# Projections multiplied by parts, score matmuls in pairs, and a reordered forget mixer with its convolution rows ranked behind the weight rests

## The chip, the cores and the metric

The kernel runs on one core of one Trainium2 chip. The metric is the device time of one execution in microseconds (us). TensorE does the matmuls, VectorE, ScalarE and GpSimd the elementwise work, and SyncE issues most transfers.

## The reference

The reference takes 256 tokens of width 1024 through three mixers and four feed-forward blocks, all in float32. The parts that matter here are these:

```python
# first mixer: differential attention (4 heads, two maps each) beside a pooling mixer
proj = rms_norm(x, norm_g) @ w_in                 # 1024 x 2048: q, k, v, u
s = einsum('bqhmd,bkhmd->bhmqk', q, k) * scale + bias      # head width 64
p = softmax(s); attn = p[:, :, 0] - lam * p[:, :, 1]
# second mixer: sliding window attention, 16 q heads, 2 kv heads, width 64, with sinks
proj = rms_norm(x, norm_g) @ w_in                 # 1024 x 1280
# third mixer ("forget mixer"), after the third feed-forward block
a, g, q, k, v, fl = split(rms_norm_2(x, mix_norm) @ w_in)  # 1024 x 2568
u = a * sigmoid(g)
y_conv = silu(layer_norm(conv31(u) + conv_b))     # 31 taps per channel, 512 channels
cum = cumsum(log_sigmoid(fl + forget_b))
s = q @ k.T * scale + cum[query] - cum[key]       # 8 heads of width 64, causal
y_attn = softmax(s) @ v
x = x + concat(rms_norm_2(y_conv), rms_norm_2(y_attn)) @ w_out
# feed-forward blocks: up to 2 x 2816, (convolution of 3 taps in the first two,) silu(gate) * up, down
```

## The kernel before

Tokens lie in two blocks of 128 (tb 0 and 1). Weights stream from memory in tiles of 1 MB (128 x 2048) in the order in which they are used (class Stream). Two staging buffers (NSTAGE) take the transfers; ScalarE rounds a staged tile into "whi" (L218) and VectorE subtracts that from the staged tile, four chunks of 512 columns, into the rest "wlo" (L222). Five buffers (NBUF) hold split tiles; one comes free when its last matmul has been done. Every float32 product is made of three matmuls of rounded numbers: activation part times weight part as hi·hi, hi·rest and rest·hi (mm3). A projection (class Proj) multiplies one token block with 512 columns of the weights in two halves of four k-blocks each; a half's weights are one tile, one chunk to a k-block.

The code states an order of work, and a planner makes each engine's order out of it at compile time: an instruction's rank is its place in the program, and on each engine the ready instruction of the best rank goes first. `tc.high_priority(offset=-n)` ranks a block as if it stood n instructions later. The split of weights stands at LATER = 400, the convolution's row steps (conv_rows) at LATERC.

Scores: a matmul of 64 rows gives one head's scores for a token block in full float32; the profile shows it as two entries. Heads (or maps) 2b and 2b+1 lie in partitions 0 to 63 and 64 to 127 of the same block. softmax_rows collects several scores of one such half in one of four PSUM buffers (pps) and lets VectorE add the bias and take the row minimum (L635) into one of six buffers "t512" (TB). In the forget mixer the function `gate` adds the cumulated gates to the scores by one matmul (L1158) and one or two more (L1160), all of 128 rows, ahead of that.

Forget mixer: conv_in(j) makes the convolution's two inputs for 128 channels, Conv.gate their product. The 31 taps are row steps on VectorE (L1088 the first, L1090 the others; 113 in all) but for 11 taps of cv[1], which TensorE does as matmuls with a diagonal (L1105) and which L1108 joins. proj_qk(s, b) makes one block of 128 rows of q (s = 0) or k (s = 1): 24 matmuls (L521 to L523) and a copy (L1148); with b = 3 it frees two weight tiles. Then come scores, transposes (values_T), products with v (values), the norms, and the out-projection in parts op.part(tb, kk): kk 2 and 3 need the attention, 0 and 1 the convolution (conv_norm, L1196 to L1204, and mix_T, whose rest part is L290).

Of the kernel before, what the change touches and what calls it, by code (L numbers as in the profile page):

```python
# [14 lines left out]
ALU = mybir.AluOpType  # L15
# [4 lines left out]
S = 256  # L20
# [17 lines left out]
NPE = (0, 11, 0, 0)  # L38
LATERC = 300
VCOPY = {((1, 0), 4), ((0, 0), 4), ((0, 1), 2), ((1, 1), 0), ((1, 1), 6)}  # L40
# [69 lines left out]
def block_kernel(ctx: ExitStack, tc: tile.TileContext, a: dict, out: bass.AP):  # L110
# [158 lines left out]
    def mm3(o, l, r, first, last):  # L269

        T.matmul(o, l[0], r[0], start=first, stop=False)  # L271
        T.matmul(o, l[0], r[1], start=False, stop=False)  # L272
        T.matmul(o, l[1], r[0], start=False, stop=last)  # L273

    def cut(pair, *idx):
# [309 lines left out]
    class Proj:  # L585
# [5 lines left out]
        def half(self, h):  # L591
            if self.o is None:
                self.o = acc_t("proj")
            w = v3(W.get(self.wname, self.first + h), 4)
            rows_mm(self.o, xT, self.tb, w, range(4 * h, 4 * h + 4), h == 0, h == 1)
            W.used(self.wname, self.first + h)
# [25 lines left out]

    def softmax_rows(qT, kT, heads, tb, rel, nm, den, SP, extra=None):

        L = P * (tb + 1)
        per = 512 // L
        for i in range(0, len(heads), per):
            pst = ps_t("sc")
            Sx = t512("S")
            for n, (r0, qb, kb, slope, idx) in enumerate(heads[i:i + per]):  # L630
                o = pst[:, n * L:(n + 1) * L]
                T.matmul(o, qT[r0:r0 + 64, qb, :], kT[r0:r0 + 64, kb, 0:L], start=True, stop=extra is None)  # L632
                if extra is not None:
                    extra(o, idx, L)
                V.tensor_tensor_reduce(Sx[:, n * L:(n + 1) * L], o, rel[:, S - L:S], slope, 3e38,  # L635
                                       ALU.add, ALU.min, nm[:, idx:idx + 1])
                SP[idx] = Sx[:, n * L:(n + 1) * L]

# [5 lines left out]
    class AttendA:  # L644
# [5 lines left out]
        def scores(self, *hs):  # L650
            tb, SP, rd, den = self.tb, self.SP, self.rd, self.den
            for m in range(2):
                softmax_rows(qTA[:, :, tok(tb)], kTA, [(64 * m, h, h, SLOPES_A[h], 2 * h + m) for h in hs],
                             tb, C("rel"), self.nm, den, SP)
            exps([2 * h + m for m in range(2) for h in hs], SP, self.nm, den)
# [259 lines left out]
    class AttendC(Values):  # L915
# [4 lines left out]
        def scores(self, *blks):  # L920
            c, tb, SP, nm, den, sk = self.c, self.tb, self.SP, self.nm, self.den, self.sk
            kT1 = kTC[c].rearrange("p (o t) -> p o t", o=1)
            for e in range(2):
                softmax_rows(qTC[c][:, :, tok(tb)], kT1,
                             [(64 * e, b, 0, SLOPES_C[8 * c + 2 * b + e], 2 * b + e) for b in blks],
                             tb, C("relw"), nm, den, SP)
            i = slice(2 * blks[0], 2 * blks[-1] + 2)
# [224 lines left out]
    class AttendF(Values):  # L1152
# [10 lines left out]
        def scores(self, *blks):  # L1163
            for e in range(2):
                softmax_rows(q2[:, :, tok(self.tb)], k2, [(64 * e, b, b, 1.0, 2 * b + e) for b in blks],
                             self.tb, C("mask"), self.nm, self.den, self.SP, self.gate)
            exps([2 * b + e for e in range(2) for b in blks], self.SP, self.nm, self.den)
            i = slice(2 * blks[0], 2 * blks[-1] + 2)
            V.reciprocal(self.rd[:, i], self.den[:, i])
# [56 lines left out]
    conv_in(3)  # L1226
    conv_rows(cv[2])
    proj_qk(1, 2)
    proj_qk(1, 1)
    proj_qk(0, 2)  # L1230
    proj_qk(1, 0)
    proj_qk(0, 3)
    cv[3].gate()
    f1.scores(0, 1)
    conv_rows(cv[3])
    f0.scores(0, 1)
    proj_qk(1, 3)
# [135 lines left out]
```

## Time and profile before

| | us |
|---|---|
| runs | 1060.22, 1063.0, 4472.5 |
| median of these | 1063.0 |
| profiled execution | 1060.59 |
| its span, first to last instruction | 1058.7 |

The profile belongs to one execution. A line of it names the engine, the line of the kernel and the tiles written and read (out<-in). PE is TensorE, PEld its weight loads, DVE VectorE, ACT ScalarE, POOL GpSimd. L12 is line 12 of the kernel. The time of a matmul in these lines is its latency; matmuls overlap, so the distance between the starts of neighbours tells what one costs in a row. Idle time before an instruction stands in brackets with what ended it.

### The profile page before, as it was taken

The numbers are of one execution on the slowest core, as the hardware profiler recorded it, in microseconds if no ns is written. First come the engines' busy times: TensorE is split into PE (matmuls) and PEld (weight loads), VectorE is DVE, ScalarE is ACT, GpSimd is POOL, SyncE is SP. The second block draws the span as 40 slices with busy tenths as digits, with TensorE's granted clock in tenths as the row PEclk, the third lists the DMA queues.
The fourth block names the chain that finished last, engine by engine and source line by source line (L and its number), as shares of the span: only waits on it lengthen the run. The fifth ranks groups of instructions, "written<-read, shape, count | busy, mean of one in ns | idle before, by whom it ended". The sixth has DMA issues, their size and how long they took to land.

```text
span 1058.7 us, 15504 instructions
## 1 busy us (share of the span) xinstructions
PE 1040.9 (98%) x5873; PEld 892.1 (84%) x5873; DVE 779.4 (74%) x1694; ACT 622.2 (59%) x1119; POOL 32.1 (3%) x40
## 2 busy tenths in 40 slices
PE   8999999999999999999999999999999999999997
PEld 5778988888877798888889888888898888888885
DVE  6686788878867578888787666656799896656662
ACT  6485666666657456666665555554644566554552
POOL 1100000000011000000000000000000010000000
PEclk9999999999999999999999999999999999999999
DMA  7635566655453074665545655554613156655531
GB/s 268 235 139 199 179 202 206 229 176 182 159 179 115 5 243 144 223 209 197 199 159 182 226 181 188 199 190 169 224 54 120 46 214 223 215 176 189 192 119 40
DMA packets 28746, 185.17 MB, mean 175 GB/s; under 512 B 3320, under 2 KB 4224, under 8 KB 7552
## 3 DMA queue, kind: packets, MB, share of 16 engines
q1 hardware_dynamic: 28672, 184.19, 50.0%
q8 instruction: 46, 0.75, 0.3%
q14 instruction: 28, 0.23, 0.1%
HBM read 183.13 MB, written 1.05 MB: 174 GB/s over the span
## 4 chain that ended last, share of the span: by engine, by line
PE 86%; DVE 6%; DMA 3%; ACT 2%; POOL 1%; issue 1%; SPq 0%; POOLq 0%; ACTq 0%; DVEq 0%
PE up L529 26%; PE up L531 14%; PE dn L271 7%; PE dn L272 7%; PE dn L273 7%; DVE wlo L222 2%; PE sc L632 2%; DMA st<-in_w 2%; PE proj L273 2%; PE o L896 2%; PE proj L272 1%; PE op L271 1%; PE op L273 1%; PE op L272 1%; PE lead L273 1%; PE lead L271 1%
## 5 line engine op out<-in xcount | busy, mean ns | idle before, releaser
L222 DVE TENSOR_TENSOR wlo<-st,whi 128x512 fp32r<-128x512 f32 x668 | 433.1, 686 | 158.2 <-ACT whi L218 158.1
L218 ACT CAST whi<-st 128x1024 fp32r<-128x1024 f32 (+1 forms) x336 | 339.1, 1042 | 131.1 <-PE dn L273 29.7
L529 PE MATMUL up<-xT,whi 128*128 128x512 f32 x1216 | 303.9, 392 | 0.8 <-DVE c L461 0.7
L529 PEld LDWEIGHTS up<-xT,whi 128*128 128x128 f32 x1216 | 220.7, 189 | 42.0 <-PE up L431 1.2
L531 PEld LDWEIGHTS up<-xT,wlo 128*128 128x128 f32 x1216 | 165.9, 190 | 11.9
L531 PE MATMUL up<-xT,wlo 128*128 128x256 f32 x1216 | 169.5, 282 | 0.0
L271 PE MATMUL dn<-whi,g 128*128 128x512 f32 x352 | 137.5, 391 | 0.0
L272 PE MATMUL dn<-wlo,g 128*128 128x512 f32 x352 | 137.1, 390 | 0.0
L273 PE MATMUL dn<-whi,g 128*128 128x512 f32 x352 | 136.7, 389 | 0.0
L536 ACT COPY h<-up 128x256 f32<-128x256 f32 x152 | 55.6, 366 | 69.3 <-PE up L531 69.0
L273 PEld LDWEIGHTS dn<-whi,g 128*128 128x128 f32 x352 | 66.1, 188 | 14.2 <-DVE g L473 0.3
L271 PEld LDWEIGHTS dn<-whi,g 128*128 128x128 f32 x352 | 66.2, 188 | 13.0 <-ACT g L472 0.4
L272 PEld LDWEIGHTS dn<-wlo,g 128*128 128x128 f32 x352 | 66.3, 188 | 12.2
L472 ACT CAST g<-m 128x256 fp32r<-128x256 f32 x88 | 35.6, 406 | 64.4 <-DVE m L468 64.4
L537 DVE TENSOR_TENSOR h<-up,h 128x256 f32<-128x256 f32 x152 | 63.6, 418 | 11.5 <-ACT h L536 11.4
L271 PE MATMUL lead<-whi,xT 128*128 128x256 f32 x192 | 55.6, 289 | 0.0
L273 PE MATMUL lead<-whi,xT 128*128 128x256 f32 x192 | 54.3, 283 | 0.0
L272 PE MATMUL lead<-wlo,xT 128*128 128x256 f32 x192 | 54.3, 283 | 0.0
L456 ACT ACTIVATE c<-h,pv 128x256 f32<-128x256 f32 x76 | 45.6, 602 | 6.1 <-DVE h L537 6.1
L473 DVE TENSOR_TENSOR g<-m,g 128x256 fp32r<-128x256 f32 x88 | 36.9, 422 | 16.5 <-ACT g L472 13.7
L272 PE MATMUL proj<-wlo,xT 128*128 128x512 f32 x112 | 44.9, 403 | 2.4 <-DVE wlo L222 2.3
L271 PE MATMUL proj<-whi,xT 128*128 128x512 f32 x112 | 44.6, 403 | 2.0 <-ACT whi L218 1.8
(227 smaller groups left out, 1366.4 us busy)
## 6 DMA issues: line engine op xcount, KB each, us to landing
st<-in_up SPq DMA_DIRECT2D x88, 1024.0 KB, 4.8
st<-in_dn SPq DMA_DIRECT2D x44, 1024.0 KB, 4.8
st<-in_w SPq DMA_DIRECT2D x21, 1024.0 KB, 4.8
gb<-in_rows SPq DMA_DIRECT2D x9, 512.0 KB, 4.2
st<-in_w0o SPq DMA_DIRECT2D x4, 1024.0 KB, 4.8
st<-in_w1o SPq DMA_DIRECT2D x4, 1024.0 KB, 4.7
st<-in_w2o SPq DMA_DIRECT2D x4, 1024.0 KB, 4.8
st<-in_w SPq DMA_DIRECT2D x4, 256.0 KB, 5.6
```

Of the source, the lines that this page charges most:

```text
L218: A.copy(hi[:, c], st[:, c])
L222: V.tensor_sub(lo[:, c], st[:, c], hi[:, c].bitcast(F32))
L271: T.matmul(o, l[0], r[0], start=first, stop=False)
L272: T.matmul(o, l[0], r[1], start=False, stop=False)
L273: T.matmul(o, l[1], r[0], start=False, stop=last)
L456: A.activation(cs[s], hs[s], AF.Identity, bias=PVs(cb, blk), scale=PVs(cw, 3 * blk + 2))
L472: A.copy(hi, m)
L473: V.tensor_sub(lo, m, hi.bitcast(F32))
L529: T.matmul(o, w[0], xT.both(ko), start=ko == 0, stop=False, skip_group_check=True)
L531: T.matmul(o[:, :S], w[1], xT[0][:, ko, :], start=False, stop=ko == KD - 1, skip_group_check=True)
L536: A.copy(h, o[:, S:])
L537: V.tensor_tensor(h, o[:, :S], h, ALU.add)
```

## The change

Proj.half no longer goes through its k-blocks with three matmuls each; mm3s makes all hi·hi products of the half, then all with the rest of the activations, then all with the rest of the weights. softmax_rows takes pairs of heads that lie in different halves of the partitions, opens two PSUM buffers at once and issues the two score matmuls of a pair one behind the other, ahead of the gates and of VectorE's reduce steps; all three mixers use it. The rank offset of the convolution's rows grows from 300 to 700. In the forget mixer the scores of the first heads move between the products of q and k, f1.scores(0, 1) is split in two, and the rows of the last convolution block come behind f1.scores(1).

```diff
--- before.py
+++ after.py
@@ -36,7 +36,7 @@
 FIRST = {("w0", 0): 4, ("w0", 1): 2}
 TB, UB = 6, 5
 NPE = (0, 11, 0, 0)
-LATERC = 300
+LATERC = 700
 VCOPY = {((1, 0), 4), ((0, 0), 4), ((0, 1), 2), ((1, 1), 0), ((1, 1), 6)}
 O_PS = {(1, 0), (1, 1)}
 DENG = "AAAA"
@@ -271,6 +271,12 @@
         T.matmul(o, l[0], r[0], start=first, stop=False)
         T.matmul(o, l[0], r[1], start=False, stop=False)
         T.matmul(o, l[1], r[0], start=False, stop=last)
+
+    def mm3s(o, terms, first, last):
+
+        order = [(l[i], r[j]) for i, j in ((0, 0), (1, 0), (0, 1)) for l, r in terms]
+        for n, (l, r) in enumerate(order):
+            T.matmul(o, l, r, start=first and n == 0, stop=last and n == len(order) - 1)
 
     def cut(pair, *idx):
         return tuple(t[idx] for t in pair)
@@ -592,7 +598,8 @@
             if self.o is None:
                 self.o = acc_t("proj")
             w = v3(W.get(self.wname, self.first + h), 4)
-            rows_mm(self.o, xT, self.tb, w, range(4 * h, 4 * h + 4), h == 0, h == 1)
+            mm3s(self.o, [(cut(xT, slice(None), 4 * h + i, tok(self.tb)), cut(w, slice(None), i)) for i in range(4)],
+                 h == 0, h == 1)
             W.used(self.wname, self.first + h)
 
         def all(self):
@@ -620,21 +627,26 @@
         A.activation((qTA, kTA)[s][:, :, tok(tb)], transposes(hn.pop((s, tb)), 4).rearrange("p (b t) -> p b t", b=4),
                      AF.Copy, scale=(nqg, PVs("kg"))[s])
 
-    def softmax_rows(qT, kT, heads, tb, rel, nm, den, SP, extra=None):
+    def softmax_rows(qT, kT, pairs, tb, rel, nm, SP, extra=None):
+
 
         L = P * (tb + 1)
         per = 512 // L
-        for i in range(0, len(heads), per):
-            pst = ps_t("sc")
-            Sx = t512("S")
-            for n, (r0, qb, kb, slope, idx) in enumerate(heads[i:i + per]):
-                o = pst[:, n * L:(n + 1) * L]
-                T.matmul(o, qT[r0:r0 + 64, qb, :], kT[r0:r0 + 64, kb, 0:L], start=True, stop=extra is None)
-                if extra is not None:
-                    extra(o, idx, L)
-                V.tensor_tensor_reduce(Sx[:, n * L:(n + 1) * L], o, rel[:, S - L:S], slope, 3e38,
-                                       ALU.add, ALU.min, nm[:, idx:idx + 1])
-                SP[idx] = Sx[:, n * L:(n + 1) * L]
+        for i in range(0, len(pairs), per):
+            pst = [ps_t("sc") for _ in range(2)]
+            Sx = [t512("S") for _ in range(2)]
+            for n, pair in enumerate(pairs[i:i + per]):
+                at = slice(n * L, (n + 1) * L)
+                for e, (r0, qb, kb, slope, idx) in enumerate(pair):
+                    T.matmul(pst[e][:, at], qT[r0:r0 + 64, qb, :], kT[r0:r0 + 64, kb, 0:L], start=True,
+                             stop=extra is None)
+                for e, (r0, qb, kb, slope, idx) in enumerate(pair):
+                    o = pst[e][:, at]
+                    if extra is not None:
+                        extra(o, idx, L)
+                    V.tensor_tensor_reduce(Sx[e][:, at], o, rel[:, S - L:S], slope, 3e38,
+                                           ALU.add, ALU.min, nm[:, idx:idx + 1])
+                    SP[idx] = Sx[e][:, at]
 
     def exps(idxs, SP, nm, den):
         for idx in idxs:
@@ -649,9 +661,8 @@
 
         def scores(self, *hs):
             tb, SP, rd, den = self.tb, self.SP, self.rd, self.den
-            for m in range(2):
-                softmax_rows(qTA[:, :, tok(tb)], kTA, [(64 * m, h, h, SLOPES_A[h], 2 * h + m) for h in hs],
-                             tb, C("rel"), self.nm, den, SP)
+            softmax_rows(qTA[:, :, tok(tb)], kTA, [[(64 * m, h, h, SLOPES_A[h], 2 * h + m) for m in range(2)] for h in hs],
+                         tb, C("rel"), self.nm, SP)
             exps([2 * h + m for m in range(2) for h in hs], SP, self.nm, den)
             i = slice(2 * hs[0], 2 * hs[-1] + 2)
             V.reciprocal(rd[:, i], den[:, i])
@@ -920,10 +931,9 @@
         def scores(self, *blks):
             c, tb, SP, nm, den, sk = self.c, self.tb, self.SP, self.nm, self.den, self.sk
             kT1 = kTC[c].rearrange("p (o t) -> p o t", o=1)
-            for e in range(2):
-                softmax_rows(qTC[c][:, :, tok(tb)], kT1,
-                             [(64 * e, b, 0, SLOPES_C[8 * c + 2 * b + e], 2 * b + e) for b in blks],
-                             tb, C("relw"), nm, den, SP)
+            softmax_rows(qTC[c][:, :, tok(tb)], kT1,
+                         [[(64 * e, b, 0, SLOPES_C[8 * c + 2 * b + e], 2 * b + e) for e in range(2)] for b in blks],
+                         tb, C("relw"), nm, SP)
             i = slice(2 * blks[0], 2 * blks[-1] + 2)
             V.tensor_tensor(nm[:, i], nm[:, i], nsink[:, 8 * c:8 * c + 8][:, i], ALU.min)
             exps([2 * b + e for e in range(2) for b in blks], SP, nm, den)
@@ -1161,9 +1171,8 @@
                          stop=kb == L // P - 1)
 
         def scores(self, *blks):
-            for e in range(2):
-                softmax_rows(q2[:, :, tok(self.tb)], k2, [(64 * e, b, b, 1.0, 2 * b + e) for b in blks],
-                             self.tb, C("mask"), self.nm, self.den, self.SP, self.gate)
+            softmax_rows(q2[:, :, tok(self.tb)], k2, [[(64 * e, b, b, 1.0, 2 * b + e) for e in range(2)] for b in blks],
+                         self.tb, C("mask"), self.nm, self.SP, self.gate)
             exps([2 * b + e for e in range(2) for b in blks], self.SP, self.nm, self.den)
             i = slice(2 * blks[0], 2 * blks[-1] + 2)
             V.reciprocal(self.rd[:, i], self.den[:, i])
@@ -1225,15 +1234,16 @@
     proj_qk(0, 1)
     conv_in(3)
     conv_rows(cv[2])
+    proj_qk(1, 1)
+    proj_qk(1, 0)
+    cv[3].gate()
+    f1.scores(0)
+    proj_qk(0, 2)
+    f1.scores(1)
+    conv_rows(cv[3])
     proj_qk(1, 2)
-    proj_qk(1, 1)
-    proj_qk(0, 2)
-    proj_qk(1, 0)
+    f0.scores(0, 1)
     proj_qk(0, 3)
-    cv[3].gate()
-    f1.scores(0, 1)
-    conv_rows(cv[3])
-    f0.scores(0, 1)
     proj_qk(1, 3)
     f1.values_T(2, 3)
     f1.scores(2, 3)
```

## Rows read from the trace of the kernel before

**Rows 1.** The page's part 1, busy us, share of the span and instructions.

```profile
PE 1040.9 (98%) x5873; PEld 892.1 (84%) x5873; DVE 779.4 (74%) x1694; ACT 622.2 (59%) x1119; POOL 32.1 (3%) x40
```

**Rows 2.** Stretches: length, busy PE, PEld, DVE, ACT, POOL, clock, DMA share, GB/s.

```profile
0.00:84.00 84.00, 77.22 (x369) 56.54 (x370) 58.81 (x163) 54.85 (x113) 9.42 (x13) 1.00 0.63 220
283.00:380.00 97.00, 96.67 (x579) 79.00 (x578) 67.43 (x186) 56.69 (x136) 10.45 (x9) 1.00 0.34 118
```

**Rows 3.** Stretches of the last mixer, same columns.

```profile
766.00:876.00 110.00, 107.83 (x739) 95.56 (x739) 102.04 (x249) 59.62 (x120) 6.22 (x8) 1.00 0.33 115
...
800.00:839.00 39.00, 38.36 (x257) 32.69 (x257) 35.35 (x110) 22.85 (x63) 0.93 (x1) 1.00 0.16 54
```

**Rows 4.** Groups of VectorE from 766 to 876 us.

```profile
L1090 DVE SCALAR_TENSOR_TENSOR ys<-u,dwh,ys 128x240 f32<-128x240 f32 (+29 forms) x109 | 44.9, 462 | 0.1
L222 DVE TENSOR_TENSOR wlo<-st,whi 128x512 fp32r<-128x512 f32 x48 | 31.8, 684 | 0.0
```

**Rows 5.** Tile proj: idle us and waits of its engine until.

```profile
  DVE wlo L222: 7.9, 14
```

**Rows 6.** Timeline of TensorE in the first mixer.

```profile
11.31 0.50 PE L272 MATMUL proj<-wlo,xT 128*128 128x512 f32 x1 [0.45 <-DVE wlo L222]
...
32.42 0.97 PE L271 MATMUL proj<-whi,xT 128*128 128x512 f32 x3 [0.80 <-ACT whi L218]
...
46.95 0.50 PE L272 MATMUL proj<-wlo,xT 128*128 128x512 f32 x1 [1.15 <-DVE wlo L222]
```

**Rows 7.** The chain that ended last, in the first mixer: start, us, what.

```profile
25.44 5.86 DMA st<-in_w
```

**Rows 8.** Timeline of TensorE, scores of the first and second mixer.

```profile
50.80 0.49 PE L632 MATMUL sc<-kTA,qTA 64*128 64x128 f32 x4
...
322.16 1.04 PE L632 MATMUL sc<-kvC,qTC 64*128 64x256 f32 x4
...
326.35 0.49 PE L632 MATMUL sc<-kvC,qTC 64*128 64x128 f32 x2
```

**Rows 9.** Timeline of TensorE, scores and gates of the last mixer.

```profile
808.71 0.70 PE L632 MATMUL sc<-qk,qk 64*128 64x256 f32 x2
809.33 0.39 PE L1158 MATMUL sc<-crow,selr 128*128 128x256 f32 x1
...
809.71 0.70 PE L632 MATMUL sc<-qk,qk 64*128 64x256 f32 x2
...
810.93 0.49 PE L632 MATMUL sc<-qk,qk 64*128 64x128 f32 x2
811.35 0.33 PE L1158 MATMUL sc<-crow,selr 128*128 128x128 f32 x1
...
811.71 0.48 PE L632 MATMUL sc<-qk,qk 64*128 64x128 f32 x2
```

**Rows 10.** Timeline of ScalarE, last rounding of the k weights.

```profile
778.09 1.04 ACT L218 CAST whi<-st 128x1024 fp32r<-128x1024 f32 x1
```

**Rows 11.** Timeline of VectorE, rests of the k weights between rows.

```profile
791.50 0.68 DVE L222 TENSOR_TENSOR wlo<-st,whi 128x512 fp32r<-128x512 f32 x1
792.10 0.45 DVE L1090 SCALAR_TENSOR_TENSOR ys<-u,dwh,ys 128x230 f32<-128x230 f32 x1
```

**Rows 12.** Timeline of TensorE in the same stretch.

```profile
792.24 0.39 PE L523 MATMUL qk<-xT,wlo 128*128 128x256 f32 x1 [0.50 <-DVE wlo L222]
...
793.21 0.39 PE L523 MATMUL qk<-xT,wlo 128*128 128x256 f32 x1 [0.35 <-DVE wlo L222]
```

**Rows 13.** Timeline of VectorE, end of the convolution and its mixed halves.

```profile
838.62 0.39 DVE L1108 TENSOR_TENSOR ys<-cv,ys 128x236 f32<-128x236 f32 x1
...
851.29 0.68 DVE L290 SCALAR_TENSOR_TENSOR mixT<-pt,mixT 128x512 fp32r<-128x512 f32 x1
...
858.63 0.68 DVE L290 SCALAR_TENSOR_TENSOR mixT<-pt,mixT 128x512 fp32r<-128x512 f32 x1
```

**Rows 14.** Groups of VectorE from 838.9 to 864.3 us.

```profile
L222 DVE TENSOR_TENSOR wlo<-st,whi 128x512 fp32r<-128x512 f32 x16 | 10.4, 684 | 0.0
```

## Prediction

> **What bounds the kernel now.** I read the page first: TensorE is busy 98% of the span, VectorE 74% [rows 1]. The four feed-forward blocks run TensorE without holes, so I went to the mixers by stretches. In the first mixer TensorE is busy 77.2 of 84 us; in the second 96.7 of 97 [rows 2]: there only shorter TensorE work can help. In the last mixer both engines are nearly full: between 766 and 876 us TensorE is busy 107.8 of 110, VectorE 102.0, so VectorE has 8.0 us to spare, 3.7 of them between 800 and 839 [rows 3]. What fills VectorE there are 109 of the convolution's 113 row steps (44.9 us) and 48 chunks of the weights' rests, "wlo" (31.8 us) [rows 4]. "Busy" of TensorE counts a matmul's whole latency, so a busy TensorE can still be slow; for that I use starts of neighbours in the timeline below.
>
> **Part 1, projections by parts.** Before, each of the four k-blocks of a half is multiplied as hi·hi, hi·rest, rest·hi, so the second matmul already wants the rest of the weights. Afterwards eight matmuls (all that use the rounded weights, whi) come first and four that use wlo last. Number and shape of matmuls, and their weight loads, stay. What it can win is waiting for wlo: the projections' tile shows 7.9 us in 14 waits over the run [rows 5], where a stop of the weight loads and one of the matmuls behind it both count. Not all of it is to be had. At the start (first half, 7 to 13 us) chunks arrive one by one; a third-block wait like the one at 11.31 (0.45 us) [rows 6] goes, but then TensorE waits for the fourth whi chunk instead, with nine or ten matmuls of 0.23 us still behind it. I worked that out as 0.3 us later for the first half, level again after the second: 0. Waits up to 32 us are paid back by the wait for whi at 32.42 (0.80 us) [rows 6], which hangs on a weight transfer that starts at 25.44 and takes 5.86 us [rows 7]; this part doesn't start it sooner: 0. Left is the wait at 46.95, 1.15 us, with some 0.1 us of slower restart [rows 6]: eight matmuls x 0.23 = 1.8 us cover it. Of this 1.2 I take 1.0, since the start of the feed-forward block behind may absorb a little. Bounds: -3.5 (under half of the doubly counted 7.9) and +0.5 (the start alone, worse than worked out).
>
> **Part 2, paired scores.** A score matmul uses 64 rows; the two of a pair use different halves of the array. The trace before shows both cases, and each score is two entries in it. In the first mixer four entries at 50.80 (two scores of 128 columns) take 0.49 us from first start to last end; in the second a lone score at 326.35, two entries, takes 0.49 as well [rows 8]. So a pair costs what one costs. In the first mixer the order already came out paired, all 16 scores: nothing is won. In the second, six scores between 326 and 335 run alone: three pairs more. One score of 128 columns holds TensorE 0.42 us (810.93 to 811.35 in the last mixer [rows 9]): 3 x 0.42 = 1.26 us. Three pairs of 256 columns are only staggered: four entries at 322.16 take 1.04 us [rows 8] where one score alone takes 0.70 (808.71 [rows 9]). Their second score waits for VectorE to empty the bank, so I count nothing for them; 3 x 0.34 = 1.0 us is the bound. TensorE is the only full engine in this stretch: -1.3, bounds 0 and -2.3.
>
> In the last mixer all 16 scores run alone, and each is followed by its gate matmuls on all 128 rows. One head of the second token block takes 1.00 us from start to start (808.71 to 809.71), of the first 0.78 (810.93 to 811.71) [rows 9]; neighbours of the former take up to 1.2, so I use 1.1. For a pair I add one score time (0.62, 808.71 to 809.33, or 0.42) and the gates once per head with one change between half and full array instead of two: estimated 1.4 and 0.95 us against 2.2 and 1.56. Four pairs of each: 4 x 0.8 + 4 x 0.6 = 5.6 us less TensorE work. At the bound they fail to form: 0.
>
> **Part 3, rows behind the rests (offset 300 to 700).** Today the rests of the k weights lie behind row steps: whi of the last of them is done at 779.13 [rows 10], but its wlo chunks run only from 791.50 on, alternating with rows [rows 11], while the k products wait for them: their third matmuls start at 792.24, 793.21 (and a third 0.97 later), each after a wait [rows 12], where three matmuls of 0.12 would make 0.36. 0.6 us three times, 0.4 around them: 2.2 us go. The same price is paid elsewhere: a row no longer done early is done later. After the convolution's last step (its join at 838.62 [rows 13]) 16 rest chunks follow before 864 [rows 14], 0.60 us apart each, 9.6 us. Five buffers hold split weights, so about ten of these (6 us) can move ahead of the rows; VectorE's 3.7 us of holes take some back. The join then comes 0 to 2.5 us later.
>
> **Part 4, the mixer's order.** Scores of the first heads go between the q and k products: the reduce step that VectorE makes of each score (L635), exponentials and transposes start some 10 us sooner and overlap the products. proj_qk is moved with its 24 matmuls and one copy of 0.38 us; the last of q frees two weight buffers, now about 4.7 us of score work later (two pairs at 1.4, two at 0.95). That holds the split and the transfer of the out-projection weights on ScalarE, VectorE and SP; they are wanted only behind the attention, some 30 us on, so 0 (2 us if that cover were gone). f1.scores(0) and (1) each take two half-used score buffers, with f0.scores(0,1) all six t512 buffers; f1.scores(2,3) then waits for the transposes of block 1, and behind it in TensorE's order stand only later transposes. One more reciprocal: 0.1 us.
>
> **What the last mixer keeps.** Parts 2 to 4 take 5.6 + 2.2 = 7.8 us from TensorE, but the end hangs on the convolution too: from the join at 838.62 the chain runs through the statistics, two normalisations and transposes to the mixed halves at 851.29 and 858.63 [rows 13], and only then the last two out-projection parts of the second block can run (12 matmuls x 0.23 = 2.7 us each). With attention done 7.8 us sooner its four parts (11 us) run before and during that chain, and after 851 four parts remain, 11 us, where now five and more do. The second half's chain also sheds some of its 16 rests. So of 7.8 I keep 3.0 (first mixed half unchanged, about one part and a little less behind it). Bounds: -7.8 (VectorE has just 8.0 us of holes) and +4.
>
> Sum: 1.0 + 1.3 + 3.0 = 5.3 us off the profiled execution, 1060.6 (span 1058.7 and 1.9 around it): 1055.3, so **1055 us**. The runs shown are 1060.2, 1063.0 and one far outlier; their median is 2.4 us above the profiled one, so a result on that level would read about 1057.5, inside the range.
>
> **Rivals.**
> - *VectorE is the wall.* The pairs feed it two banks at once, each head costs 0.2 to 0.35 us of it, and it has no time: the last mixer gives 0, the others 2.3: 1058. For it: 102 of 110 us busy. Against: some of its holes are waits for TensorE's scores, which go. The Trainium skill, "TensorEngine Tiling (Array Packing)", section "PSUM Bottleneck", speaks for this rival: packing makes TensorE faster and not the emptying of PSUM, so by it the sum would be this 1058; no row of the trace before shows paired scores beside the convolution's rows.
> - *Both follow in full.* Rests come early, rows fill only holes: 7.8, with 2.3 in the second mixer and 3.0 in the first: 13.1 off, 1047.5.
> - *The convolution comes last* (other side). All 16 rests pass the rows: the join at 838.62 + 9.6 - 3.7 = 844.5, 5.9 later, and the tail, a chain over four engines, stays as long. Minus 2.3 from the other mixers: +3.6, 1064. It decides once the join is more than 2.3 us late and the tail doesn't shrink. For it: the rows lose rank and VectorE is full. Against: five weight buffers stop the rests.
> - *The pairs don't form* in the second and last mixer (four PSUM buffers, six score buffers), while the k rests do come early: 1.0 + 1.0: 1058.5.
>
> **How the numbers follow.** Forecast (1050 to 1057.5) 0.45; VectorE the wall or no pairs 0.25; both in full 0.15; convolution last 0.15. The range reaches to the middle of the last two: 1047 to 1064, which holds eight cases in ten once noise of some 2 us is added. Two per cent, 21 us, is about what a measurement of this kernel can tell from no change; no case reaches it: faster 0.03, same 0.95, slower 0.02.
>
> **What would show it.** Right: no wait for wlo in the projections at 47 us; scores of the last mixer in fours (two entries doubled), their total busy time down by about 4; no wait of the k products for wlo; join of the convolution at about the same time before the mixer's end as now or less; last mixer 3 us shorter, the second 1.3. Wrong: TensorE idle for several us before the first mixed half (convolution last), row steps after all out-projection parts, or the feed-forward start waiting for its weights by as much as the mixer won.

## The result: 1071.6 us, 0.9% slower

The changed kernel takes 1071.6 us (median of 20 runs, 1069.2 to 1074.3), the kernel before 1061.7 in the same comparison; the ratio is 1.0094 with a 95% interval of 1.0084 to 1.0104. I had forecast 1055 in a range of 1047 to 1064: outside the range, on the other side of no change, and still within the two per cent that I gave 0.95. Executions of one kernel differ: 20 of the kernel before, timed beside the first experiments, took 1059.4 to 1073.2 us at mean granted clocks of 0.999 to 0.986, and every length below is that of one profiled execution.

### The profile page after: what moved, and what is told of

Same layout as the page of the kernel before. It is cut to its first block, busy times and chain, and to the rows that moved or that the text cites. A ratio compares the mean times of both kernels' runs of the same rounds, so it can differ in the third digit from the quotient of the medians.

```text
span 1070.0 us, 15517 instructions
## 1 busy us (share of the span) xinstructions
PE 1044.9 (98%) x5873; PEld 896.3 (84%) x5873; DVE 781.5 (73%) x1695; ACT 622.5 (58%) x1119; POOL 31.5 (3%) x40
## 4 chain that ended last, share of the span: by engine, by line
PE 85%; DVE 7%; DMA 3%; ACT 2%; POOL 1%; issue 1%; SPq 0%; POOLq 0%; ACTq 0%
PE up L535 26%; PE up L537 14%; PE dn L271 7%; PE dn L272 7%; PE dn L273 7%; PE proj L279 4%; DVE ys L1100 2%; DVE wlo L222 2%; DMA st<-in_w 2%; PE lead L271 2%; PE lead L273 2%; PE lead L272 2%; PE op L271 2%; PE op L273 2%; PE op L272 2%; PE sc L641 2%
## 5 line engine op out<-in xcount | busy, mean ns | idle before, releaser
L279 PE MATMUL proj<-whi,xT 128*128 128x512 f32 x224 | 61.0, 403 | 4.1 <-ACT whi L218 2.3
L279 PEld LDWEIGHTS proj<-whi,xT 128*128 128x128 f32 x224 | 40.4, 188 | 16.4 <-ACT whi L218 5.1
```

The source lines that it names most:

```text
L279: T.matmul(o, l, r, start=first and n == 0, stop=last and n == len(order) - 1)
```

## The profile after

The page's first part has the same load as before [rows 1], in a longer span (1070.0 us); the row of the granted clock in 40 slices has an 8 where the kernel before had nines throughout:

```profile
span 1070.0 us, 15517 instructions
...
PE 1044.9 (98%) x5873; PEld 896.3 (84%) x5873; DVE 781.5 (73%) x1695; ACT 622.5 (58%) x1119; POOL 31.5 (3%) x40
...
PEclk9999999999999999999999999999998999999999
```

Where the time went is read from landmarks. In every run I take the first mixer from the start of the span to the start of its last matmul, and the other two from the start of the last down-product ahead of them to the start of the first matmul of the next feed-forward block. First mixer: 100.3 us before, 101.3 after. Second mixer: 86.2, 86.1. Last mixer (746.7 to 865.4 in the kernel before): 118.7 before, 129.9 after. The feed-forward blocks differ by about half a microsecond at most. So the last mixer lost 11.2 us, the first 1.0, and the second won nothing.

Stretches of the last mixer; the first two answer to [rows 3], the others are short pieces inside (columns as there, the granted clock third from the end):

```profile
766.00:876.00 110.00, 100.20 (x649) 87.60 (x648) 95.27 (x237) 53.50 (x110) 4.47 (x7) 0.94 0.32 111
800.00:839.00 39.00, 35.58 (x224) 30.75 (x224) 35.20 (x107) 22.14 (x57) 0.00 (x0) 0.87 0.28 95
810.00:817.00 7.00, 5.86 (x24) 5.29 (x25) 5.41 (x21) 2.81 (x9) 0.00 (x0) 0.54 0.01 2
825.00:832.00 7.00, 5.99 (x32) 5.17 (x30) 6.15 (x19) 6.39 (x16) 0.00 (x0) 0.76 0.22 90
855.00:860.00 5.00, 2.62 (x12) 1.84 (x10) 3.90 (x8) 5.00 (x7) 0.93 (x1) 1.00 0.00 0
860.00:865.00 5.00, 3.79 (x12) 2.91 (x13) 4.95 (x11) 1.25 (x3) 0.55 (x1) 0.68 0.74 264
```

VectorE, which I had called full (102.0 of 110 us), is now busy for 95.3 of them, TensorE for 100.2 instead of 107.8, and TensorE's clock is at half (1.2 instead of 2.4 GHz) in three places. Counted over time, one minus the granted clock adds up to 6.8 us over this mixer; I call that its lost clock. In the profiled execution of the kernel before it was 0.

The groups of VectorE from 766 us to the convolution's last step: up to 838.9 us before (first fence; the last step there is the join), up to 851.9 after:

```profile
L222 DVE TENSOR_TENSOR wlo<-st,whi 128x512 fp32r<-128x512 f32 x22 | 15.0, 683 | 0.0
L635 DVE CUSTOM_DVE_ANT_0 S<-sc,cc 128x256 f32<-128x256 f32 (+1 forms) x16 | 5.4, 355 | 2.1 <-PE sc L1160 1.1 <-PE cv L1105 0.9
```

```profile
L1100 DVE SCALAR_TENSOR_TENSOR ys<-u,dwh,ys 128x247 f32<-128x247 f32 (+26 forms) x109 | 45.3, 462 | 0.5
L222 DVE TENSOR_TENSOR wlo<-st,whi 128x512 fp32r<-128x512 f32 x33 | 21.0, 683 | 2.6 <-ACT whi L218 2.6
L647 DVE CUSTOM_DVE_ANT_0 S<-sc,cc 128x256 f32<-128x256 f32 (+1 forms) x16 | 5.4, 350 | 3.0 <-PE sc L1170 3.0
```

The same 109 rows [rows 4], but 33 rest chunks ahead of the last step instead of 22. One of the 33 began ahead of 766 us and only ends behind it; counted from the mixer's start the chunks are 37 before and 47 after. So ten more pass: at 0.60 us of distance 6.0 us. VectorE also stands still longer, for a rounded tile (2.6 us, before none) and for scores (3.0 instead of 2.1).

The four largest waits of TensorE between 766 and 876 us, in all, times, longest:

```profile
PE pt L549 <- DVE mv L1206: 2.9, 1, 2.9
PE sc L641 <- DVE nm L647: 2.0, 1, 2.0
PE pt L549 <- DVE z L1187: 1.5, 2, 1.3
PE op L271 <- ACT mixT L295: 1.4, 2, 0.7
```

No wait of the k products for wlo is left: they had three of 0.35 to 0.50 us [rows 12]. In their place stand the two longest, of 2.0 and 2.9 us. The timeline of TensorE around them:

```profile
807.86 0.49 PE L641 MATMUL sc<-qk,qk 64*128 64x128 f32 x4
...
808.78 0.33 PE L527 MATMUL qk<-xT,whi 128*128 128x256 f32 x1
811.14 0.79 PE L641 MATMUL sc<-qk,qk 64*128 64x128 f32 x2 [2.03 <-DVE nm L647]
...
857.23 0.39 PE L273 MATMUL op<-whi,mixT 128*128 128x512 f32 x1
860.52 0.63 PE L549 MATMUL pt<-cc,z 128*128 128x128 f32 x4 [2.91 <-DVE mv L1206]
861.84 0.79 PE L271 MATMUL op<-whi,mixT 128*128 128x512 f32 x1 [0.69 <-ACT mixT L295]
862.43 0.63 PE L272 MATMUL op<-wlo,mixT 128*128 128x512 f32 x1
```

The scores do pair (four entries in 0.49 us at 807.86, where two took that long [rows 9]). The second pair waits 2.0 us for VectorE's reduce step and comes apart (six of this mixer's eight pairs form), and behind that wait a score of two entries takes 0.79 us, not 0.49: half clock. At 857.2 all out-projection parts that need no convolution are done; TensorE waits 2.9 us for the first normalised half, and behind that the out-projection's matmuls take 0.63 us instead of 0.39. The fall between these two, at 827.6, stands behind a wait of 1.0 us at 827.2 for ScalarE. The timeline of VectorE shows the late convolution itself; the join, its last step before [rows 13], no longer is the last:

```profile
847.95 3.91 DVE L1100 SCALAR_TENSOR_TENSOR ys<-u,dwh,ys 128x233 f32<-128x233 f32 x8
852.28 1.30 DVE L1205 BATCH_NORM_STATS2 st<-yT 128x6 f32<-128x512 f32 x2 [0.42 <-PE yT L1201]
...
861.82 0.69 DVE L296 SCALAR_TENSOR_TENSOR mixT<-pt,mixT 128x512 fp32r<-128x512 f32 x1
...
870.58 0.69 DVE L296 SCALAR_TENSOR_TENSOR mixT<-pt,mixT 128x512 fp32r<-128x512 f32 x1 [0.24 <-ACT mixT L295]
```

Eight rows in 3.91 us, 0.49 us each, since one convolution block is left and each of its steps waits for the one before; with rows of two blocks in turn they come every 0.39 us. The mixed halves come 10.5 and 12.0 us later than before [rows 13].

In the first mixer the wait for wlo at 46.95 [rows 6] is gone, and another, for ScalarE's copy of k, has come. The scores behind it start at 50.80, as before [rows 8]; before, all of them ran in fours, and here four of them run alone. TensorE after, and the first scores of 256 columns before:

```profile
50.80 0.49 PE L641 MATMUL sc<-kTA,qTA 64*128 64x128 f32 x4 [1.11 <-ACT kTA L627]
...
52.97 0.48 PE L641 MATMUL sc<-kTA,qTA 64*128 64x128 f32 x2
...
53.81 0.48 PE L641 MATMUL sc<-kTA,qTA 64*128 64x128 f32 x2
...
58.61 0.70 PE L641 MATMUL sc<-kTA,qTA 64*128 64x256 f32 x4
```

```profile
57.65 0.70 PE L632 MATMUL sc<-kTA,qTA 64*128 64x256 f32 x4
```

From the first score to those of 256 columns it takes 7.8 us instead of 6.85: the 1.0 us that this mixer lost.

## The experiments

Three theories: **R**, the rests pass the rows, so that the convolution comes last; **O**, the new order of the mixer does that by itself; **P**, the pairs cost VectorE and the PSUM buffers more than they give. Later **K** came: part of the loss is the clock. All results in one table (ratio to the kernel before; lengths and lost clock in us, worked out from each run's trace as above):

| kernel | ratio, 95% interval | first mixer | last mixer | its lost clock | last less lost |
|---|---|---|---|---|---|
| before | 1 | 100.3 | 118.7 | 0 | 118.7 |
| changed | 1.0094, 1.0084 to 1.0104 | 101.3 | 129.9 | 6.8 | 123.1 |
| before_rank700 | 1.0133, 1.0115 to 1.0151 | 99.9 | 134.7 | 12.0 | 122.7 |
| before_order | 0.9993, 0.9973 to 1.0013 | 100.2 | 119.7 | 0 | 119.7 |
| before_parts | 1.0038, 1.0010 to 1.0066 | 107.1 | 119.0 | 0 | 119.0 |
| before_pairs | 0.9979, 0.9961 to 0.9996 | 99.9 | 118.7 | 0 | 118.7 |
| after_rank300 | 1.0042, 1.0025 to 1.0059 | 101.3 | 122.4 | 3.4 | 119.0 |
| pairs_order | 0.9992, 0.9980 to 1.0004 | 100.0 | 119.1 | 0 | 119.1 |
| order_rank700 | 1.0088, 1.0068 to 1.0108 | 100.1 | 130.8 | 6.8 | 123.9 |
| after_no_parts | 1.0076, 1.0059 to 1.0093 | 99.8 | 130.3 | 6.8 | 123.5 |
| rests_later_too | 1.0017, 1.0006 to 1.0029 | 103.8 | 120.2 | 1.7 | 118.5 |
| pairs_order_rank500 | 1.0080, 1.0050 to 1.0109 | 100.9 | 129.5 | 6.8 | 122.7 |
| pairs_rank100 | 1.0070, 1.0046 to 1.0093 | 100.1 | 126.7 | 5.1 | 121.6 |
| filled | 1.0080, 1.0068 to 1.0092 | 103.3 | 127.4 | 5.1 | 122.3 |
| filled_four | 1.0069, 1.0047 to 1.0092 | 102.3 | 125.0 | 0 | 125.0 |
| pairs_taps15 | 1.0002, 0.9994 to 1.0011 | 100.5 | 121.4 | 0 | 121.4 |
| pairs_taps8 | 1.0009, 0.9990 to 1.0029 | 100.3 | 122.3 | 1.7 | 120.6 |
| pairs_late_parts | 0.9995, 0.9980 to 1.0009 | 100.4 | 118.7 | 0 | 118.7 |
| rests_gpsimd | 1.0090, 1.0056 to 1.0123 | 100.0 | 131.1 | 10.2 | 120.9 |
| pairs_rests_gpsimd | 1.0036, 1.0016 to 1.0056 | 100.0 | 126.2 | 5.1 | 121.0 |

### One edit at a time

```diff
-LATERC = 700          # after_rank300: the changed kernel with
+LATERC = 300
-LATERC = 300          # before_rank700: the kernel before with
+LATERC = 700
```

> The changed kernel with only the convolution's rank offset back at 300. Theory R (the rests pass the rows, so the convolution comes last): the last row step, 12.8 us later in the changed kernel, comes back to within 3 us of the kernel before, the 3.1 us wait ahead of the mixed halves is gone, and the time is 1058 to 1063 us. Theory O (the new order puts the last block's rows too late, whatever the offset): rows still end more than 8 us late and the time stays at 1068 or above. Theory P (paired scores cost VectorE and the score buffers more than they give TensorE): likewise 1068 or above, with waits of the score matmuls for VectorE.

> The kernel before with only the offset 700. Theory R: the k products no longer wait for the rests, the rows end 8 to 13 us later, the last mixer is 8 to 12 us longer: 1069 to 1073 us. Theories O and P: within 2 us of the kernel before, 1059 to 1064.

before_order takes the new lines of the mixer's order alone, before_parts mm3s in Proj.half alone, before_pairs the new softmax_rows and its three calls alone.

> The kernel before with only the new order of the forget mixer (scores alone, offset 300). Theory O: rows end 8 to 13 us later and the time is 1068 to 1072. Theories R and P: within 3 us of the kernel before, 1059 to 1065.

> The kernel before with only the projections by parts. If the loss of 1.0 us that the changed kernel shows ahead of the first feed-forward block is this edit's: first mixer +1.0 us, the others within 0.3, the time +1 us (ratio 1.000 to 1.002). If it is the pairs': first mixer unchanged or 1 us shorter as predicted, ratio 0.998 to 1.000. The last mixer unchanged by both.

> The kernel before with only the scores in pairs (offset 300, old order, projections as before). My prediction's part 2: second mixer 1.3 us shorter, last mixer 3 to 5.6 us shorter: 1055 to 1059. Theory P (a pair takes two of the four PSUM buffers at once and waits for VectorE's reduce steps, and such a wait can bring the granted clock down): score matmuls wait over 1 us at least once, the granted clock falls to half for some us in the last mixer, last mixer 2 to 4 us longer: 1061 to 1066.

The offset alone costs 15.9 us of last mixer (the convolution's last step ends 16.1 us later after the mixer's start), more than the whole change and more than the 8 to 12 us that R expected. O and P fall: order and pairs alone change the time by 0.2% at most. after_rank300 is not quite back: its convolution ends 3.3 us late, and in its trace the clock is at half from 825 to 832 (3.4 us lost); less that, its mixer is as long as before.

The parts were the surprise. The wait for k's copy that the changed kernel has at 50.80 is here, too, a little longer, and what follows is the fall of the clock. Timeline of TensorE, and a stretch behind it:

```profile
52.25 0.49 PE L639 MATMUL sc<-kTA,qTA 64*128 64x128 f32 x4 [1.39 <-ACT kTA L627]
...
53.81 1.22 PE L279 MATMUL proj<-wlo,xT 128*128 128x512 f32 x2
```

```profile
54.00:64.00 10.00, 10.00 (x23) 6.21 (x24) 4.95 (x21) 5.15 (x16) 0.00 (x0) 0.51 0.35 129
```

Ten microseconds at half clock, 5.1 lost, of the 6.8 by which this first mixer is longer. The other runs with the parts throughout have first mixers of 101.3 (changed, after_rank300) and 102.3 to 103.8 (three with 1.7 us lost between 9 and 15 us); those without stay at 99.8 to 100.9. In all six with the parts throughout the same four scores of the first mixer run alone, in none of the others.

### Which part of the loss goes with which edit

```diff
 pairs_order:    paired softmax_rows + new order, offset 300, no mm3s
 order_rank700:  new order + LATERC = 700
 after_no_parts: the changed kernel without mm3s
```

> The kernel before with paired scores and the new order (offset 300, projections as before). It is the earlier run at offset 300 without the parts. If the pairs make its last mixer 3.7 us longer: the same here, with a stretch of half clock; first mixer without the loss of 1 us and the time 1063 to 1065. If the parts made it: the last mixer is back at 119 to 120 us and the time at 1060 to 1062.

> The kernel before with the new order and the offset 700, scores alone. Together with the run of offset 700 alone and the next one it tells what brings the loss of 15.9 us (offset alone) down to 11.2 (the whole change). If the order does it: last mixer 129 to 131 us, time 1070 to 1072. If the pairs do it: last mixer 133 to 136, time 1074 to 1077.

> The changed kernel without the projections by parts. If these cost 1.0 us at the start and nothing in the last mixer: first mixer as before, last mixer 129 to 131 us as in the changed kernel, time 1069 to 1071. If they also touch the last mixer's split and rows: last mixer off by over 1.5 us either way.

The four kernels with the offset 700 so far have last mixers of 129.9 to 134.7 us, lone or paired, with the parts or without; the five with 300 (before among them) 118.7 to 119.7, but for after_rank300 with its lost clock, 122.4. The order takes 3.9 us off the loss of the offset alone, and 5.1 us less of its clock is lost, so by itself it gains nothing there; the pairs take nothing off (130.8, 130.3). The waits of TensorE in pairs_order between 766 and 876 us say where the pairs' gain went:

```profile
PE pt L543 <- DVE z L1180: 1.7, 2, 1.2
PE sc L634 <- DVE nm L640: 1.4, 2, 0.9
PE qk L523 <- DVE wlo L222: 1.2, 3, 0.5
```

From start to start, scores and gates of this mixer took TensorE 14.8 us before and take 10.6 here, with six of the eight pairs formed; in before_pairs, the old order, four form and it takes 12.4. Of the 4.2 us some 2.5 show as new waits for VectorE (1.4 us for reduce steps, before none; 1.7 for normalised halves, before 0.6), and the mixer is as long as it was.

### The rank of the rests against that of the rows

```diff
+    W.later = 800      # rests_later_too: the changed kernel, split at this offset in the last mixer
-LATERC = 300           # pairs_order_rank500: pairs_order with
+LATERC = 500
-LATERC = 300           # pairs_rank100: before_pairs with
+LATERC = 100
```

> The changed kernel, but in the last mixer the weights' split has its offset raised too (400 to 800), so that rows and rests stand to one another about as before. Theory R1 (what counts is that the rests pass the rows): the last mixer comes back to 118.5 to 121 us, the time to 1060 to 1063 us. Theory R2 (what counts is that the rows go behind all other work of VectorE): the last mixer stays at 126 us or more, the time at 1067 or above. The first mixer keeps its loss of 1.0 us in both.

> Paired scores and the new order with the offset 500 instead of 300 or 700 (119.06 and 130.31 us of last mixer). If the loss jumps where rows fall behind the rests (400): 128 to 131 us. If it grows with the offset: 122 to 127. If only the last steps up to 700 hurt: 119 to 121.

> The kernel before with paired scores and the offset 100 instead of 300, so that rows go further ahead of the rests: the mixer's optimum looked for on the other side. If the convolution's end sets the mixer's length: rows end 1 to 3 us sooner and the last mixer takes 116 to 118 us. If the rests are then late for the k products and the attention: those wait longer than the 2.2 us so far, and the mixer takes 120 us or more. If nothing hangs on it any more: 118.3 to 119.2.

With the rows left at 700 and the rests moved behind them, the last mixer is back at 120.2 us: what counts is who passes whom (R1). The time, 1063.8 us, is above R1's range, by less than what the first mixer lost (103.8 instead of 100.3). At 500 the loss is nearly all there, so it comes with the change of ranks and not step by step. At 100 the rests are too late instead: TensorE's longest wait for them is this one, against 0.5 us before [rows 12]:

```profile
810.14 0.58 PE L523 MATMUL qk<-xT,wlo 128*128 128x256 f32 x1 [4.03 <-DVE wlo L222]
```

### Keeping the clock up

```diff
-    f0.scores(0, 1)                    # filled: the changed kernel with matmuls of zeros
+    f0.scores(0)
+    keep_busy(8, acc_t("idle"))
+    f0.scores(1)
...
     op.part(1, 3)
+    keep_busy(14)
     op.part(1, 0)
...
+    keep_busy(8, acc_t("idle"))        # filled_four: these two too, further up
     f1.scores(2, 3)
...
+    keep_busy(6, acc_t("idle"))
     f1.values(2, 3)
```

> The changed kernel with 22 matmuls of zeros that nothing reads: 8 ahead of the scores before which TensorE waits 2.2 us for VectorE (and after which its granted clock falls), 14 ahead of the out-projection parts that wait for the convolution. Lost clock so far: the sum over the last mixer of one minus the granted clock is 6.8 us of its 129.9. Theory K (rows late by 4 to 5 us, the rest is the clock): the falls behind these two places go, lost clock 0 to 3 us, last mixer 123 to 126.5 us. Theory R alone (the late convolution explains all 11.2 us, the clock falls only where TensorE would wait anyway): last mixer 129 to 131 us even where the clock stays up.

> The changed kernel with matmuls of zeros that nothing reads at four places of the last mixer (those of the run with two, and ahead of the second block's last scores and values, where the clock then fell). Theory K (rows late 4 to 5 us, the rest lost clock): with a lost clock of 0 to 2 us the last mixer takes 121.5 to 125 us; in any case its length less the lost clock is 121.5 to 124. Theory R alone: 127 to 130 us with the clock kept up.

With two fillers the falls at 810 and 861 are gone, but TensorE now waits 2.1 us ahead of the second block's scores, and the clock is at half from 823 to 833 (5.1 us lost): the mixer takes 127.4 us, in neither theory's range. With four the clock stays up in this mixer throughout. Stretches of filled_four, to be read against those of the changed kernel above, and the pair that waited there:

```profile
766.00:876.00 110.00, 104.75 (x717) 89.60 (x720) 98.98 (x245) 56.20 (x115) 4.44 (x7) 1.00 0.31 111
805.00:815.00 10.00, 9.46 (x74) 8.24 (x73) 10.00 (x32) 3.27 (x9) 0.00 (x0) 1.00 0.01 2
```

```profile
811.23 0.49 PE L641 MATMUL sc<-qk,qk 64*128 64x128 f32 x4
```

With the 36 matmuls that do nothing the mixer is 4.9 us shorter (125.0). The rows end 6.6 us sooner, with the same 47 chunks ahead of them and 5.4 us less idle time of VectorE: it had been standing behind a slow TensorE. So, on these two traces, about 4.9 of the 11.2 us go with the clock (K), and 6.3 with VectorE's order by itself. K had the mixer less its lost clock at 121.5 to 124, R alone the mixer at 127 to 130; 125.0 lies between.

Two things weaken this. The edit also splits f0.scores(0, 1), so that the second pair has buffers of its own: it comes as a pair, without the wait of 2.0 us, and no run has the split without the fillers. And over all executions the gain is not clear of noise: a ratio of 1.0069 (1.0047 to 1.0092) against 1.0094 (1.0084 to 1.0104). The table's last column, 122 to 124 us for the six kernels at 500 or 700 that lost clock, would leave only 4 to 5 for the order; I can't decide between the two, as the fillers take TensorE's time too.

### What swallows the pairs' gain

```diff
-NPE = (0, 11, 0, 0)    # pairs_taps15, pairs_taps8: before_pairs with
+NPE = (0, 15, 0, 0)    # taps(7), taps(5), taps(3)
+NPE = (0, 8, 0, 0)     # taps(4), taps(3), taps(1)
-V.tensor_sub(lo[:, c], ...)                                      # both _gpsimd
+(G if key[0] == "w2o" and q % 2 else V).tensor_sub(lo[:, c], ...)
+if self.wname == "w0" and self.first >= 4:   # pairs_late_parts: mm3s there only
```

> The kernel before with paired scores (last mixer 118.71 us, the same as without pairs) and 15 instead of 11 taps of the second convolution block on TensorE: 4 row steps of 0.385 us fewer for VectorE, 4 matmuls of 0.4 us more for TensorE. If VectorE and the convolution are the wall that swallowed the pairs' TensorE time: last mixer 117.0 to 118.2, time 1058 to 1060. If TensorE is: last mixer 119.5 to 121. If neither (the tail's chain alone): 118.4 to 119.2.

> The kernel before with paired scores and 8 instead of 11 taps of the second convolution block on TensorE: 3 row steps more for VectorE (1.2 us), 3 matmuls of two entries fewer for TensorE (1.2 us). If the join that waits for the last taps leads the tail (15 taps: 2.7 us longer): last mixer 117 to 118.3 us, time 1058 to 1060. If VectorE is the wall: 119.5 to 120.5.

> The kernel before; 8 rest chunks of the out-projection weights of the last mixer (0.6 us each on VectorE) are made by GpSimd. If VectorE is the wall: rows and normalisations end 2 to 5 us sooner, last mixer 114 to 117.5 us, time 1057 to 1060. If the chain behind the attention and the taps' join is: 118 to 119.2 us. If GpSimd's chunks take over 2 us each or slow VectorE's own work beside them: 120 us or more.

> The same with paired scores. If VectorE was what swallowed the pairs' gain: 1 to 4 us shorter than the run with lone scores, last mixer 112 to 116.5 us. If not: the same as that within 0.5 us.

> The kernel before with paired scores, and only the first mixer's third and fourth projection by parts (the first two, whose chunks arrive one by one, as before; those of the other mixers as before too). If my part 1 was right but for the start: the wait for the rests at 46.95 us goes and the first mixer takes 98.7 to 99.2 us instead of 99.9, time 1058 to 1060. If the wait only moves to the scores behind the projections (1.28 us at 50.6 in the changed kernel): 99.7 to 101.5.

Taps moved either way make the mixer longer, by 2.7 and 3.6 us: with 15 the join that waits for TensorE's taps comes 3.2 us later than in before_pairs, with 8 the last row 4.5 (and 1.7 us of clock are lost, behind a wait of 1.9 us for rests). With 8 the mixer is longer than either case expected. As I read it, neither engine alone is the wall. In before_pairs the last row ends 92.8 us and the join 92.4 us after the mixer's start, so the convolution stands split where both end together (without pairs the last row ends at 88.4), and TensorE time saved elsewhere in the mixer shortens neither side.

Work taken off VectorE by GpSimd was lost, for the two hold each other up. VectorE and GpSimd of pairs_rests_gpsimd, in that order:

```profile
801.82 1.52 DVE L1093 SCALAR_TENSOR_TENSOR ys<-u,dwh,ys 128x252 f32<-128x252 f32 x1
803.26 1.77 DVE L222 TENSOR_TENSOR wlo<-st,whi 128x512 fp32r<-128x512 f32 x1
...
805.75 6.66 DVE L1093 SCALAR_TENSOR_TENSOR ys<-u,dwh,ys 128x250 f32<-128x250 f32 x17
```

```profile
807.99 5.55 POOL L222 TENSOR_TENSOR wlo<-st,whi 128x512 fp32r<-128x512 f32 x1 [3.50 <-ACT whi L218]
```

A row beside a GpSimd chunk takes 1.52 us instead of 0.48, a rest chunk 1.77 instead of 0.68; and a GpSimd chunk that falls into 17 rows in a row takes 5.55 us, where the shortest takes 1.27. The Trainium skill, "SBUF — State Buffer", section "SBUF: two separate sides", says why: an operation of VectorE with two inputs from SBUF and one of GpSimd that reads there share a port pair that one of them holds for its whole instruction. The trace agrees. So this pair of runs doesn't answer whether VectorE alone swallows the gain: the pairs shorten this mixer by 5.0 us (131.1 to 126.2), and all of that is lost clock (10.2 to 5.1).

pairs_late_parts kept the start in the old order, and its wait for the rests at 47 us stayed, 0.8 us, so the parts don't cover it there. No version is shown to beat the kernel before; the pairs alone come nearest (0.2%, with an interval that ends at 0.9996, in one of nineteen comparisons).

## Why the prediction was wrong

**The failed step is in part 3: "The join then comes 0 to 2.5 us later."** The convolution's last step comes 12.3 us later after the mixer's start. The count that I began with was right: about ten chunks pass the rows, and ten did; they make 5.8 of the 12.3 us. Wrong was what I set against it. "VectorE's 3.7 us of holes take some back": holes are where VectorE waits for TensorE or ScalarE, its order is fixed, and with TensorE late they grew, by 3.4 us from the mixer's start to that last step (and to 15 us instead of 8 between 766 and 876). The rest I didn't see: 2.0 us of the attention's normalisations and mixed halves that now come ahead of the last rows, and 1.1 us because the last block's rows, alone, cost 0.49 us each instead of 0.39.

**The rival "the convolution comes last" had the mechanism, and its price without the clock:** 5.9 us for the mixer, where the run with the clock kept up shows 6.3. That the two are so near is luck: the rival lets all 16 chunks pass and takes 3.7 us of holes off, while ten passed and no hole took anything off. I gave it 0.15, arguing that five weight buffers stop the rests; ten passed all the same, and by its own account the rival needed only 2.3 us of lateness.

**What no case had is the clock.** All rows of before showed 1.00, and I took matmul prices as fixed. A change that makes TensorE wait 1 to 3 us in a mixer where it had waited 0.6 at most put three falls of the clock into it, 6.8 us, and with the clock kept up the mixer was 4.9 us shorter (with the two reservations above). The Trainium skill, "TensorE: Matmul & The Clock Gate", section "Part 1: The HAM clock gate", has the clock follow the engine's recent activity; the runs agree, in that it stayed at 1.00 through filled_four's last mixer with fillers that compute nothing.

**Part 2.** The TensorE time was about right (4.2 us saved in the last mixer with the order, 5.6 forecast for pairs that all form), but "what the last mixer keeps" was not 3.0 but 0: 118.71 us with and without pairs, 119.06 and 119.67 in the new order. That is the rival "VectorE is the wall", as far as the size goes; the runs with other taps point rather to two ends that stand level. The Trainium skill, "TensorEngine Tiling (Array Packing)", section "PSUM Bottleneck", says that packed matmuls go faster while the emptying of PSUM does not; the runs agree as far as scores now wait 1.4 us for the reduce steps that empty their banks. The second mixer, where only TensorE is full, gave nothing of my 1.3 us either (85.8 to 86.2 us in the runs with lone scores, 84.8 to 87.6 with pairs). There the rival "the pairs don't form" came true: in before_pairs the same six scores that ran alone before run alone still, two of them here, and all of this mixer's scores take TensorE 10.9 us from start to start in both:

```profile
325.12 0.48 PE L634 MATMUL sc<-kvC,qTC 64*128 64x128 f32 x2
...
325.91 0.48 PE L634 MATMUL sc<-kvC,qTC 64*128 64x128 f32 x2
```

The price itself was right. In filled, where all of them came out paired, they take 9.6 us and the mixer 84.8, 1.3 less than before. Why the planner pairs them there and not in before_pairs isn't shown.

**Part 1.** The wait at 46.95 went, as forecast, and behind it TensorE was 1.4 us ahead. But the scores then wait for k and start at 50.80 as before, so the 1.0 us that I took was not won. What I had put at nothing is the order of the scores among the projection's matmuls: four of them lose their partners and cost the 1.0 us. The start is not the place. Waits of the projections' tile for wlo (7.9 us in 14 [rows 5]) became waits for whi (4.8 us in 6 before, 7.5 in 12 after), but at 44.5 us both kernels stand at the same matmul. In place of -1.0 stand +1.0 (changed against before) to +1.5 (changed against after_no_parts, where 0.4 us more lies ahead of the scores), and +6.8 in before_parts, where the clock falls. The bound of +0.5 was too narrow.

**Part 4** counted nothing for the order, and alone it changes nothing that can be told from noise: 0.9993 of before (0.9973 to 1.0013).

Of the signs that I named, three came true (no wait at 47 us, four entries to a pair for six of eight pairs, no wait of the k products), and so did the first one named for wrong, TensorE idle for several us before the first mixed half. The scores' total busy time fell by 1.9 us (15.7 to 13.8), not by 4.

## What to carry to other kernels

When work of two ranks shares an in-order engine, moving one past the other isn't a shift into holes: count the chunks that pass, and take the whole sum as the least delay of the other (here 5.8 us of chunks, 12.3 of delay). Where two engines ended a stage level, as here, time taken off one of them bought nothing, and work moved either way cost. Before counting on two matmuls to run as a pair, find out whether the plan puts them next to each other; here a change elsewhere made pairs and broke them. And before an edit adds waits to TensorE, price the half clock behind them as well: here 6.8 us were lost to it in the last mixer.

## What the runs showed of the hardware

- TensorE's granted clock fell to half behind waits of 0.6 us (after_rank300, at 822.5), 1.4 us (first mixer of before_parts, 5.1 us lost), 1.0, 2.0 and 2.9 us (changed kernel), but not behind 1.1 us at 50.80 and 1.3 us at 844.1 of the changed kernel or 1.8 us at 822.8 of filled_four. The waits alone don't sort the cases; what else counts stays open.
- Idle matmuls may pay: with 36 of them, and one call of scores split in two, the last mixer was 4.9 us shorter in the trace; over all executions the gain is not clear of noise.
- Two scores of 64 rows and 128 columns that lie in different halves of the partitions took 0.49 us side by side (50.80 in the first mixer), as long as one alone; four that lost their partners cost the first mixer 1.0 us.
- VectorE and GpSimd, both on SBUF: a row step went from 0.48 to 1.52 us beside a GpSimd chunk, and a GpSimd chunk from 1.27 to 5.55 us among rows.
